# Logits from the unnormed residual, four largest marked by matching, and the first expert's rows gathered in float32

## The chip, the cores and the metric

The kernel runs on one core of one Trainium2 chip. The metric is the device time of one execution in microseconds. The engines are PE (TensorE, matmuls; PEld is its weight load), DVE (VectorE), ACT (ScalarE), POOL (GpSimd) and SP (SyncE, which here issues the large loads). Line numbers L… are those of the kernel before unless "of after" is said.

## What is computed

One block with 256 tokens of width 1024, all in float32: embedding layer norm, a mixer of three branches (sparse attention, S5 scan, attention to a memory) whose gated sum goes through w_o, a DeepNorm residual with layer norm, a mixture of 32 experts of which each token takes four, and a second residual with layer norm. The part that the change touches, in the reference, shortened:

```python
h = _layer_norm(DEEPNORM_ALPHA * h + mix, ln1_g[l], ln1_b[l])
...
logits = xt @ w_router + b_router
top_val, top_idx = lax.top_k(logits, TOP_K)
gate = jax.nn.softmax(top_val, axis=-1)
...
g, lin = jnp.split(xb @ w_gate_up[e] + b_gate_up[e], 2, axis=-1)
act = min(g, 7) * sigmoid(1.702 * min(g, 7)) * (clip(lin, -7, 7) + 1)
y = act @ w_down[e] + b_down[e]          # weighted by gate, summed per token
...
h = _layer_norm(DEEPNORM_ALPHA * h + ffn, ln2_g[l], ln2_b[l])
```

The expert weights are 32 × (8 + 4) MB: the bulk of all that is read.

## The kernel before

**Tiles.** The 256 tokens are two tiles (t = 0, 1) of 128 rows, one token to a partition; the width of 1024 is 8 k-tiles of 128 columns. `h` [128, 2, 1024] holds the residual stream, and is also the accumulator `acc` of the experts.

**Weights.** They come as chunks of 1 MB, [128, 2048] float32. An expert has 8 chunks of w_gate_up and 4 of w_down, 384 in all. Chunks and large intermediate tiles share slots of 8 KB a partition in four pools (tags u, w, s, z with 13, 3, 4 and 4 slots; `PATTERN` says which tag the next chunk takes, `WHERE` where a large tile goes). All loads are issued on SP's queue in program order (L76), so a load whose slot is still in use stops every load behind it. The intermediates `xT1` (transposed rows for the router), `r` (remainder of the split, below) and `l1s` (gain and bias of the layer norm, spread) lie in slots of tag s, and `hb01` in one of tag z, and so each of them delays the chunk that takes its slot next. Some chunks are loaded ahead of the routing (`load_some`).

**Order.** The code is written engine by engine in program order, and a tile scheduler reorders within what the dependencies allow; `issue_after` holds a group of instructions back until a named one stands.

**Before the experts.** `project` multiplies the merged mixer output with w_o into PSUM banks `pz` (L203 to L205, products of the parts hl, mgTh, mgTl, into which both operands are split). The spreads (L141, L913) put the norm's gain and bias on all partitions as `l1s`. Then, for each tile: the residual is added (L921), statistics are taken (L922 to L925, `inv_sqrt` L108 to L117 is a Newton iteration on DVE), h is normalised in place on DVE (L928), 8 transposes (L224) and a copy give `xT1`, and the router multiplies: 8 float32 matmuls with the router weights as the stationary operand in strips of 32 columns (L935), a copy (L938), one matmul by `stack` that adds the strips (L940), and the bias (the norm's gain and bias are folded into the router weights beforehand).

**Routing.** L946 to L953: the eight largest by max, their positions by max_index, a uint32 to float32 cast (L948), a comparison with `eio` (0 to 31) for the first four, and a sum over the four: `sel`, and `selb` in bf16. A matmul by a triangular matrix `before` (L957), for tile 1 with one by ones (L956) ahead of it, counts the earlier tokens of each expert; `posm` (L959, L960) is a token's slot in its expert, or a large number where it isn't marked. Beside it: softmax of the four (`e`, L964 to L967), put in place by `eq` (`gmat`, L969), and `count`, the number of tokens of each expert (L983, L984).

**The split.** h is split into three bf16 parts that add up to it: hi = bf16(h) and mid = bf16(h − hi) on ACT (L977), with r = h − hi and the last part by subtractions of which the first is on DVE and three on POOL (`SUBS`, "VGGG"). The parts lie in `hb01` (hi and mid), `hb2` and the end of the tile `bias`.

**One expert** (`expert`, 64 slots): one-hot `oh` and `og` from posm (L1020, L1021); 48 bf16 matmuls (8 k-tiles, 3 parts, 2 token tiles) gather its rows transposed into PSUM `xg` (L1028); a multiplication on DVE and an addition on POOL apply the layer norm's gain and bias (`xT`); `pw`, `ohT` and `gs` (L1038 to L1042) serve the way back; bias products with `sel` (L1049, L1089); up (L1049, 8 chunks, into pg and pl), swiglu, transposes, down (L1094, 4 chunks), and the combination into acc (L1109, added on DVE). An expert's gathers stand on PE ahead of the up products of the expert before.

**Callbacks.** Expert 0 calls `residual` once xT is written: h is multiplied by alpha and by l1s's gain, and its bias added (L988 to L993, four pieces each). Expert 1 calls `further_blocks`: from `count` it works out how many further blocks of 64 slots an expert needs (`nblk`, L998 to L1003), which each engine, SP among them, reads into a register (TENSOR_LOAD, L1163) to branch over the extra blocks.

Of the kernel before, what the change touches and what calls it, by code (L numbers as in the profile page):

```python
# [52 lines left out]
SUBS = "VGGG"  # L53
L1B = ["mm", "sc", "mm", "sc"]
# [4 lines left out]
def block_kernel(ctx: ExitStack, tc: tile.TileContext, a: dict, out: bass.AP):  # L59
# [33 lines left out]
    G.iota(slot, pattern=[[0, 2], [1, CAP]], base=0, channel_multiplier=0, allow_small_or_imprecise_dtypes=True)  # L93
    posm = cp.tile([128, NT, NE], F32)
# [6 lines left out]
    late = cp.tile([128, 1], F32)  # L101

# [76 lines left out]
    with ExitStack() as fx:  # L179
# [587 lines left out]
        tt(brt, brt, pb_[:, :NE], OP.add)  # L767

# [90 lines left out]
        eio = fp.tile([128, NE], F32)  # L859
        G.iota(eio, pattern=[[1, NE]], base=0, channel_multiplier=0, allow_small_or_imprecise_dtypes=True)  # L860
# [54 lines left out]
        for t in range(NT):  # L915
            zt = h[:, t, :]
            hs = [(slice(n * 512, (n + 1) * 512), zt[:, n * 512:(n + 1) * 512]) for n in range(2)]

            bs = f2.tile([128, 2, 6], F32, tag="bs", name="bs")
            for n, (sl, zh) in enumerate(hs):  # L920
                V.scalar_tensor_tensor(zh, pz[t][n], 0.5 / ALPHA, zh, op0=OP.mult, op1=OP.add)  # L921
                V.bn_stats(bs[:, n, :], zh)  # L922
            mv = f2.tile([128, 2], F32, tag="mv", name="mv")
            V.bn_aggr(mv, bs.rearrange("p a b -> p (a b)"))
            V.tensor_scalar(mv[:, 1:2], mv[:, 1:2], LN_EPS / ALPHA ** 2, None, op0=OP.add)  # L925
            rs = inv_sqrt(f2, mv[:, 1:2])
            for sl, zh in hs:
                V.tensor_scalar(zh, zh, mv[:, 0:1], rs, op0=OP.subtract, op1=OP.mult)  # L928
            transpose_rows(zt, xT1, t, tag="mm" if t else "tr", eng=V if t else None)


            p = bank("mm" if t else "tr")
            for k in range(KT):
                j = k % 4
                PE.matmul(p[32 * j:32 * j + 32, :128], wr[:, k, :], xT1[:, k, t * 128:(t + 1) * 128],  # L935
                          start=k < 4, stop=k >= 4)
            lt = f2.tile([128, 128], F32, tag="lt", name="lt")
            S.activation(lt, p[:, :128], AF.Copy)  # L938
            p = bank("mm" if t else "tr")
            PE.matmul(p[:, :NE], lt, stack, start=True, stop=True)  # L940
            lgt = f2.tile([128, NE], F32, tag="lgt", name="lgt")
            tt(lgt, p[:, :NE], brt, OP.add)
            v8 = f2.tile([128, 8], F32, tag="v8", name="v8")
            i8 = f2.tile([128, 8], U32, tag="i8", name="i8")
            f8 = f2.tile([128, 8], F32, tag="f8", name="f8")
            V.max(v8, lgt)  # L946
            V.max_index(i8, v8, lgt)
            V.tensor_copy(f8, i8)  # L948
            eq = f2.tile([128, 4, NE], F32, tag="eq", name="eq")
            sel = f2.tile([128, NE], F32, tag="sel", name="sel")  # L950
            tt(eq, eio[:, None, :].to_broadcast([128, 4, NE]), f8[:, 0:4, None].to_broadcast([128, 4, NE]), OP.is_equal)
            V.tensor_reduce(sel, eq.rearrange("p k e -> p e k"), axis=AX.X, op=OP.add)
            V.tensor_copy(selb[:, t, :], sel)  # L953
# [5 lines left out]
            V.scalar_tensor_tensor(posm[:, t, :], sel, -1e6, p[:, :NE], op0=OP.mult, op1=OP.add)  # L959
            V.tensor_scalar(posm[:, t, :], posm[:, t, :], 1e6, None, op0=OP.add)  # L960

            e4 = f2.tile([128, 4], F32, tag="e4", name="e4")
            nm = f2.tile([128, 2], F32, tag="nm", name="nm")
            V.tensor_scalar(nm[:, 0:1], v8[:, 0:1], -1.0, None, op0=OP.mult)  # L964
            S.activation(e4, v8[:, 0:4], AF.Exp, bias=nm[:, 0:1], accum_out=nm[:, 1:2])
            V.reciprocal(nm[:, 1:2], nm[:, 1:2])
            V.tensor_scalar(e4, e4, nm[:, 1:2], None, op0=OP.mult)  # L967
            tt(eq, eq, e4[:, :, None].to_broadcast([128, 4, NE]), OP.mult)
            V.tensor_reduce(gmat[:, t, :], eq.rearrange("p k e -> p e k"), axis=AX.X, op=OP.add)  # L969


        for t in range(NT):
            zt, rt = h[:, t, :], r[:, t, :]
# [36 lines left out]
    def expert(mp, pm, gu, dn, pick_e, pos_e, gate_e, slots, then=None, last=None, after=None):  # L1010
# [22 lines left out]
        if then:  # L1033
            then(xT[:, KT - 1, 0:1])
# [265 lines left out]
```

## Time and profile before

| what | us |
|---|---|
| three runs | 1274.22, 1274.98, 1280.77 |
| median | 1274.98 |
| profiled execution, device time | 1278.62 |
| its span in the trace | 1276.9 |
| PE busy in the span | 1217.3 (95%) |
| DVE, ACT, POOL busy | 582.5, 283.5, 63.3 |

The profiled execution is the one that the rows of the trace tell of; it took 3.64 us longer than the median, and 1.7 us of its device time lie outside the span. Times in rows are microseconds from the span's start. Each timeline row gives start, busy time, engine, line, operation, what is written and read, tile shapes, and in brackets how long the engine had been idle before it and what ended that wait. SPq rows are load issues. Equal rows that lie close together are counted as x2, x4 and so on.

### The profile page before, as it was taken

The page shows a single profiled execution, that of the slowest core. Times are in us where ns is not written, and L with a number is a line of the kernel's source. Part 1 is how long each engine was busy: PE and PEld are TensorE (multiplying, and loading weights), DVE is VectorE, ACT ScalarE, POOL GpSimd, SP SyncE. Part 2 cuts the span into 40 slices and gives each one's busy share as a digit, 9 for nine tenths or more (in the row PEclk, how much of TensorE's full clock was granted, in tenths as well). Part 3 has the DMA queues.
Part 4 walks back from the last instruction along what each step waited for, and adds up shares of the span by engine and source line. Part 5 has one row for each costly group of instructions (what it writes and reads, how often), then busy time and mean ns, then how long its engine had stood idle before and what let it go on. Part 6 is the DMA issues. An engine that isn't in the chain of part 4 may idle for free. (4 is left out here: it accounts for less than half of the span.)

```text
span 1276.9 us, 17711 instructions
## 1 busy us (share of the span) xinstructions
PE 1217.3 (95%) x7277; PEld 616.7 (48%) x7278; DVE 582.5 (46%) x1168; ACT 283.5 (22%) x513; POOL 63.3 (5%) x104
## 2 busy tenths in 40 slices
PE   7999999999799999999999999999999999999995
PEld 6657898789533343444444444433333333333341
DVE  5599986657733343333433333333333333333325
ACT  4346469864201110000101001001100000001011
POOL 1000000000200000000000000000000000000000
PEclk9999989999799999999999999999999999999998
DMA  7335546447789999999999999999999999999993
GB/s 273 109 126 198 180 151 215 165 148 282 296 360 427 427 426 427 426 427 426 426 426 427 426 427 425 427 426 427 428 427 425 427 426 427 426 427 427 426 427 143
DMA packets 65333, 451.95 MB, mean 354 GB/s; under 512 B 8896, under 2 KB 9056, under 8 KB 11360
## 3 DMA queue, kind: packets, MB, share of 16 engines
q1 hardware_dynamic: 64960, 450.26, 85.7%
q8 instruction: 58, 0.95, 0.3%
q10 hardware_dynamic: 288, 0.52, 0.1%
q14 instruction: 27, 0.22, 0.0%
HBM read 449.70 MB, written 1.05 MB: 353 GB/s over the span
## 5 line engine op out<-in xcount | busy, mean ns | idle before, releaser
L1049 PE MATMUL pg<-w,xT 128*64 128x512 f32 x1024 | 294.0, 605 | 8.0 <-DMA w<-in_w_gate_up 8.0
L1049 PE MATMUL pl<-w,xT 128*64 128x512 f32 x1024 | 285.6, 592 | 0.0
L1094 PE MATMUL py<-w,aT 128*64 128x512 f32 x1024 | 240.5, 598 | 15.8 <-DMA w<-in_w_down 15.8
L80 DVE TENSOR_TENSOR h<-h,pc 128x512 f32<-128x512 f32 x128 | 82.2, 683 | 267.4 <-PE pc L1109 267.4
L1049 PEld LDWEIGHTS pl<-w,xT 128*64 128x64 f32 x1024 | 95.4, 137 | 126.7 <-issue 103.4
L1069 ACT ACTIVATE sg<-gc 128x512 f32<-128x512 f32 x32 | 20.2, 630 | 560.6 <-DVE gc L1068 560.6
L1094 PEld LDWEIGHTS py<-w,aT 128*64 128x64 f32 x1024 | 69.6, 136 | 154.0 <-issue 100.3
L1049 PEld LDWEIGHTS pg<-w,xT 128*64 128x64 f32 x1024 | 75.3, 136 | 119.6 <-DMA w<-in_w_gate_up 54.7
L1101 DVE SCALAR_TENSOR_TENSOR ys<-py,gs,ys 128x512 fp32r<-128x512 f32 x64 | 48.0, 751 | 166.0 <-ACT ys L1100 162.6
L1100 ACT ACTIVATE ys<-py,gs 128x512 fp32r<-128x512 f32 x64 | 44.0, 687 | 240.6 <-PE py L1094 240.6
L1109 PE MATMUL pc<-ys,ohT 128*128 128x512 f32 x256 | 77.0, 422 | 0.9 <-DVE h L80 0.8
L1109 PEld LDWEIGHTS pc<-ys,ohT 128*128 128x128 f32 x256 | 42.9, 188 | 57.8 <-issue 50.7
L191 DVE TENSOR_TENSOR hl<-w,hl 128x1024 fp32r<-128x1024 f32 x48 | 58.1, 1219 | 17.7 <-ACT hl L190 17.5
L83 POOL TENSOR_TENSOR xT<-xT,lc 128x512 f32<-128x512 f32 x32 | 41.3, 1291 | 472.3 <-DVE xT L80 472.3
L1028 PEld LDWEIGHTS <-hb 128*128 128x128 bf16 x1280 | 47.3, 98 | 30.2 <-issue 28.3
L205 PE MATMUL mm<-hTh,hl 128*128 128x256 f32 x192 | 56.3, 293 | 0.0
L203 PE MATMUL mm<-hTh,hl 128*128 128x256 f32 x192 | 56.2, 293 | 0.0
L204 PE MATMUL mm<-hTl,hl 128*128 128x256 f32 x192 | 55.7, 290 | 0.0
L1068 DVE TENSOR_SCALAR gc<-pg 128x512 f32<-128x512 f32 x32 | 22.1, 691 | 69.9 <-PE pg L1049 69.9
L190 ACT ACTIVATE hl<-w 128x1024 fp32r<-128x1024 f32 x48 | 49.8, 1053 | 18.1 <-PE mm L205 12.5
L1028 PE MATMUL xg<-oh,hb 128*128 128x64 bf16 x1280 | 52.3, 194 | 1.5 <-DVE oh L1020 0.9
L1041 DVE TENSOR_SCALAR ohT<-pw 128x256 fp32r<-128x256 f32 x32 | 13.6, 424 | 71.0 <-PE pw L1038 71.0
(396 smaller groups left out, 1484.0 us busy)
## 6 DMA issues: line engine op xcount, KB each, us to landing
w<-in_w_gate_up SPq DMA_DIRECT2D x256, 1024.0 KB, 19.6
w<-in_w_down SPq DMA_DIRECT2D x128, 1024.0 KB, 19.6
w<-in_w_g SPq DMA_DIRECT2D x12, 1024.0 KB, 4.9
w<-in_w_s_glu SPq DMA_DIRECT2D x4, 1024.0 KB
w<-in_w_o SPq DMA_DIRECT2D x4, 1024.0 KB, 4.7
w<-in_w_memk SPq DMA_DIRECT2D x2, 1024.0 KB, 10.7
w<-in_w_u SPq DMA_DIRECT2D x2, 1024.0 KB, 8.9
w<-in_w_memv SPq DMA_DIRECT2D x2, 1024.0 KB, 5.1
```

The source lines that it names most:

```text
L80: V.tensor_tensor(o, x, y, op=op)
L190: S.activation(hi, src, AF.Copy)
L191: (eng or V).tensor_tensor(lo, src, hi.bitcast(F32), op=OP.subtract)
L203: PE.matmul(o, lhsT(0), rhs(0), start=start, stop=False)
L204: PE.matmul(o, lhsT(0), rhs(1), start=False, stop=False)
L205: PE.matmul(o, lhsT(1), rhs(0), start=False, stop=stop)
L1028: PE.matmul(xg[:, k, :], hb[t][b][:, k * 128:(k + 1) * 128], oh[:, t, :], start=n == 0, stop=n == 5)
L1049: m = PE.matmul(p_[hf * 64:(hf + 1) * 64, :], lhsT, w[:, o + hf * 512:o + (hf + 1) * 512], start=start, stop=stop)
L1094: end = PE.matmul(py[j * 64:(j + 1) * 64, :], a4[:, k // 4, k % 4 + j, :], dn(k + j, hf), start=k + j == 1, stop=k == 6)
L1100: S.activation(y2[:, 0], py, AF.Copy, scale=gs)
L1101: V.scalar_tensor_tensor(y2[:, 1], py, gs, y2[:, 0].bitcast(F32), op0=OP.mult, op1=OP.subtract)
L1109: PE.matmul(pc, ohT[:, t * 128:(t + 1) * 128], ys[hf][:, i], start=i == 0, stop=i == 1)
```

## The change

**Logits.** The residual add, transposes, copy and router products now go by halves of 512 columns (`half(t, n)`), on the residual that isn't normalised yet, with xT1 as the stationary operand (128 columns) and the router weights moving (32 columns): 8 matmuls of 128x32 a tile into one bank `raw`, no strips and no `stack` product. `route(t)` applies mean and deviation to the logits: (raw − mean · swr) · rs + brt, where swr, made once beforehand, holds the column sums of the router weights on all partitions. h is normalised in place by ACT. Tile 0's halves stand between the projections of tile 1, tile 1's first half between those of its second.

**Marking.** max gives the eight largest; match_replace puts 3e38 where one of the first four stands (the eight slots are filled up with −3e38, which the four columns beyond the 32 logits hold), and a comparison gives `selb` at once. `slot` is 1e6 smaller, so that posm needs no second operation.

**What moved behind.** `gates` (softmax over the marked logits) is issued behind expert 0's one-hots. `residual`, issued behind expert 0's last gather matmul, now also allocates r, hb01 and l1s, makes the three bf16 parts (for experts 1 to 31; ACT copies, all four subtractions on DVE) and the spreads of l1s. `further_blocks` counts the marked tokens itself, behind expert 1's gather.

**Expert 0's rows** are gathered from h in float32: 16 matmuls (8 k-tiles, 2 token tiles) with h as the stationary operand, into xg and one `pc` bank; the gain and bias are applied by DVE (k-tiles 0 to 3) and ACT (4 to 7). The down bias products of every expert stand behind its transposes.

SP's queue around the routing: loads of weight chunks, with the semaphores that each waits for (DMAHW: an older load has landed; PE, DVE, Pool, Activation: that engine's last use of the slot). Before, from the 18th chunk on:

```order
89 L76 DMA w<-in_w_gate_up 128x2048 [waits DMAHW3_49]
90 L76 DMA w<-in_w_down 128x2048 [waits DVE_49,DMAHW4_49,PE_49,Activation_49]
91 L76 DMA w<-in_w_down 128x2048 [waits DMAHW5_49,Pool_49]
92 L1163 TENSOR_LOAD nblk [waits DVE_49]
93 L1163 ISA x2
94 L76 DMA w<-in_w_gate_up 128x2048 [waits DMAHW6_49,PE_49]
95 L76 DMA w<-in_w_gate_up 128x2048 [waits DMAHW7_49,PE_49]
```

Row 90 takes xT1's slot, row 91 that of r, and row 94 that of expert 0's first chunk. After:

```order
90 L74 DMA w<-in_w_gate_up 128x2048 [waits DMAHW5_49,PE_49]
91 L74 DMA w<-in_w_down 128x2048 [waits DMAHW6_49,DVE_49]
92 L74 DMA w<-in_w_gate_up 128x2048 [waits DMAHW7_49,PE_49]
93 L74 DMA w<-in_w_gate_up 128x2048 [waits DMAHW0_49,PE_49]
94 L74 DMA w<-in_w_gate_up 128x2048 [waits DMAHW1_49,PE_49]
95 L74 DMA w<-in_w_gate_up 128x2048 [waits DMAHW2_49,PE_49]
96 L74 DMA w<-in_w_gate_up 128x2048 [waits DMAHW3_49,PE_49]
97 L74 DMA w<-in_w_down 128x2048 [waits DMAHW4_49,DVE_49,Activation_49]
98 L74 DMA w<-in_w_gate_up 128x2048 [waits DMAHW5_49,PE_49]
99 L74 DMA w<-in_w_down 128x2048 [waits DMAHW6_49,PE_49]
100 L74 DMA w<-in_w_gate_up 128x2048 [waits DMAHW7_49,PE_49]
101 L1210 TENSOR_LOAD nblk [waits DVE_49]
```

Row 90, the 20th chunk, takes the slot of expert 0's first chunk; row 91, the 21st, takes r's slot, now behind DVE; row 97 takes l1s's slot. The read of nblk has moved from behind the 20th chunk to behind the 30th.

DVE's list from expert 0's way back on. Before:

```order
499 L1041 TENSOR_SCALAR ohT<-pw 128x256
500 L1042 TENSOR_REDUCE gs<-pw 128x1
501 L1021 TENSOR_SCALAR og<-slot,posm,gmat 128x128 x2
502 L1020 TENSOR_SCALAR oh<-slot,posm 128x64
503 L988 TENSOR_SCALAR late<-xT 128x1
504 L80 TENSOR_TENSOR xT<-xg,lc 128x512
505 L992 SCALAR_TENSOR_TENSOR h<-h,late,l1s 128x512 x4
506 L1020 TENSOR_SCALAR oh<-slot,posm 128x64 x2
507 L993 SCALAR_TENSOR_TENSOR h<-l1s,h 128x512 x4
```

And after (hb_3131 is hb01, hb_77 is hb2, the third part of tile 0; bias holds that of tile 1):

```order
487 L995 TENSOR_SCALAR late<-xT 128x1
488 L1086 TENSOR_SCALAR ohT<-pw 128x256
489 L1087 TENSOR_REDUCE gs<-pw 128x1
490 L1051 TENSOR_SCALAR og<-slot,posm,gmat 128x128 x2
491 L78 TENSOR_TENSOR r<-h,hb_3131 128x1024 x2
492 L1008 SCALAR_TENSOR_TENSOR h<-h,l1s 128x512
493 L78 TENSOR_TENSOR hb_77<-r,hb_3131 128x1024
494 L1008 SCALAR_TENSOR_TENSOR h<-h,l1s 128x512
495 L78 TENSOR_TENSOR bias<-r,hb_3131 128x1024
496 L1008 SCALAR_TENSOR_TENSOR h<-h,l1s 128x512 x2
497 L1009 SCALAR_TENSOR_TENSOR h<-l1s,h 128x512 x4
```

Before, DVE has no part of the split here, and expert 1's xT (row 504) stands in between; after, the four subtractions are interleaved with l1s's products, and expert 1's rows come later.

PE's list of after from the last projection products to the first expert weights:

```order
1177 L208 MATMUL av<-hl,mgTl 128x512
1178 L927 MATMUL mm<-ident,h 128x128 x4
1179 L933 MATMUL sc<-s_w_router,xT_2867 128x32 x8
1180 L927 MATMUL mm<-ident,h 128x128 x4
1181 L933 MATMUL sc<-s_w_router,xT_2867 128x32 x8
...
1187 L957 MATMUL mm<-selb,before 128x32
1188 L1060 MATMUL xg<-oh,h 128x64 x16
1189 L144 MATMUL pc<-gbin_ln_g,ident 128x128 x4
1190 L1083 MATMUL pw<-ident,og 128x128 x2
...
1199 L1094 MATMUL pg<-w,xT 64x512 x2
```

Before, the same stretch held four spreads, two times 8 transposes, two times 8 router matmuls with a stack product, one gather matmul, and the bias products, and then 47 more gather matmuls of expert 0 and all 48 of expert 1 ahead of the first product with expert weights; now expert 1's gathers stand behind expert 0's up products.

The diff, cut to what the text speaks of:

```diff
-SUBS = "VGGG"
-L1B = ["mm", "sc", "mm", "sc"]
...
+    V.tensor_scalar(slot, slot, -1e6, None, op0=OP.add)
...
+        wrs = fp.tile([128, NE], F32)
+        V.tensor_reduce(wrs, wr.rearrange("p k e -> p e k"), axis=AX.X, op=OP.add)
...
+        PE.matmul(pb_[:, :NE], onesf, wrs, start=True, stop=True)
+        swr = fp.tile([128, NE], F32)
+        S.activation(swr, pb_[:, :NE], AF.Copy)
...
-        for n in range(2):
-            for k in range(2, KT):
-                project(1, n, k)
-        l1s = big("l1s", [128, 4, 512], **at("l1s"))
-        for i in range(4):
-            S.activation(l1s[:, i], spread(gb1, i, bank(L1B[i], BANKS[L1B[i]])), AF.Copy)
...
+        def half(t, n):
+            zh = h[:, t, n * 512:(n + 1) * 512]
+            V.scalar_tensor_tensor(zh, pz[t][n], 0.5 / ALPHA, zh, op0=OP.mult, op1=OP.add)
+            p = bank("mm" if t else "tr")
+            for k in range(4):
+                PE.transpose(p[:, k * 128:(k + 1) * 128], zh[:, k * 128:(k + 1) * 128], ident)
+            S.activation(xT1[:, 4 * n:4 * n + 4, t * 128:(t + 1) * 128], p.rearrange("p (k c) -> p k c", k=4), AF.Copy)
+            V.bn_stats(stats[t][:, n, :], zh)
...
+            for k in range(4 * n, 4 * n + 4):
+                PE.matmul(raw[t][:, :NE], xT1[:, k, t * 128:(t + 1) * 128], wr[:, k, :], start=k == 0, stop=k == KT - 1)
...
+            V.scalar_tensor_tensor(lgt, swr, nmr[:, 0:1], raw[t][:, :NE], op0=OP.mult, op1=OP.add)
+            V.scalar_tensor_tensor(lgt, lgt, rs, brt, op0=OP.mult, op1=OP.add)
...
+                S.activation(zh, zh, AF.Identity, scale=rs, bias=nmr[:, 1:2])
+            V.max(top[t][:, 0:8], lgt)
...
+            V.match_replace(mark, top[t].rearrange("p (a b) -> p a b", b=4)[:, 0:3:2, :], lg[t], 3e38)
+            V.tensor_scalar(selb[:, t, :], mark[:, :NE], 3e38, None, op0=OP.is_equal)
...
+        for k in range(2, KT):
+            project(1, 0, k)
+        for n in range(2):
+            half(0, n)
+        route(0)
+        for k in range(2, 5):
+            project(1, 1, k)
+        half(1, 0)
+        for k in range(5, KT):
+            project(1, 1, k)
+        half(1, 1)
+        route(1)
...
     def residual(x):
-        V.tensor_scalar(late, x, ALPHA, ALPHA, op0=OP.min, op1=OP.max)
+        r = big("r", [128, NT, D], **at("r"))
+        hb01 = big("hb01", [128, 2, NT, D], BF, tag="z", bufs=NZ)
...
+        V.tensor_scalar(late, x, 1.0, 1.0, op0=OP.min, op1=OP.max)
         for t in range(NT):
             zt, rt = h[:, t, :], r[:, t, :]
...
+            S.activation(hb[t][0], zt, AF.Copy, scale=late)
+            tt(rt, zt, hb[t][0], OP.subtract)
+            S.activation(hb[t][1], rt, AF.Copy)
+            tt(hb[t][2], rt, hb[t][1], OP.subtract)
+        l1s = big("l1s", [128, 4, 512], **at("l1s"))
+        for i in range(4):
+            S.activation(l1s[:, i], spread(gb1, i, pm.tile([128, 512], F32, tag="pc", name="pc", bufs=2)), AF.Copy)
...
+        if first:
+            xg1 = pm.tile([128, 512], F32, tag="pc", name="xg", bufs=2)[:, :256].rearrange("p (k c) -> p k c", k=4)
+            for k in range(KT):
+                o = xg[:, k, :] if k < 4 else xg1[:, k - 4, :]
                 for t in range(NT):
-                    PE.matmul(xg[:, k, :], hb[t][b][:, k * 128:(k + 1) * 128], oh[:, t, :], start=n == 0, stop=n == 5)
+                    after = PE.matmul(o, h[:, t, k * 128:(k + 1) * 128], oh[:, t, :], start=t == 0, stop=t == 1)
...
         if then:
-            then(xT[:, KT - 1, 0:1])
+            with tc.issue_after(after.ins):
+                then(xT[:, KT - 1, 0:1])
```

More of the change, by code (lines that the diff above doesn't have):

```diff
@@ L101, in block_kernel @@
     late = cp.tile([128, 1], F32)
+    one = cp.tile([128, 1], F32)
+    G.memset(one, 1.0)
+    lg = [cp.tile([128, NE + 4], F32, name=f"lg{t}") for t in range(NT)]
+    top = [cp.tile([128, 12], F32, name=f"top{t}") for t in range(NT)]
     def inv_sqrt(st, v, n=1):
@@ L929, in block_kernel @@
[L929 to L953, printed above, removed]
+            lgt = lg[t][:, :NE]
+            V.scalar_tensor_tensor(lgt, swr, nmr[:, 0:1], raw[t][:, :NE], op0=OP.mult, op1=OP.add)
+            V.scalar_tensor_tensor(lgt, lgt, rs, brt, op0=OP.mult, op1=OP.add)
@@ L966, in block_kernel @@
-            V.reciprocal(nm[:, 1:2], nm[:, 1:2])
-            V.tensor_scalar(e4, e4, nm[:, 1:2], None, op0=OP.mult)
-            tt(eq, eq, e4[:, :, None].to_broadcast([128, 4, NE]), OP.mult)
-            V.tensor_reduce(gmat[:, t, :], eq.rearrange("p k e -> p e k"), axis=AX.X, op=OP.add)
+            V.scalar_tensor_tensor(posm[:, t, :], selb[:, t, :], -1e6, p[:, :NE], op0=OP.mult, op1=OP.add)
+        for k in range(2, KT):
+            project(1, 0, k)
+        for n in range(2):
+            half(0, n)
@@ new lines, in block_kernel, with gates @@
+        route(0)
[6 more added lines that the diff above has]
+        route(1)
+    hb = []
+    def gates(mp):
+        w = mp.tile([128, 512], F32, tag="lin", name="ex", bufs=1).rearrange("p (i e) -> p i e", e=NE)
+        for t in range(NT):
+            ex, sel, nm = (w[:, 3 * t + i, :] for i in range(3))
+            V.tensor_scalar(nm[:, 0:1], top[t][:, 0:1], -1.0, None, op0=OP.mult)
+            S.activation(ex, lg[t][:, :NE], AF.Exp, bias=nm[:, 0:1])
+            V.tensor_scalar(sel, posm[:, t, :], 0.0, None, op0=OP.is_lt)
+            tt(ex, ex, sel, OP.mult)
+            V.tensor_reduce(nm[:, 1:2], ex, axis=AX.X, op=OP.add)
+            V.reciprocal(nm[:, 1:2], nm[:, 1:2])
+            V.tensor_scalar(gmat[:, t, :], ex, nm[:, 1:2], None, op0=OP.mult)
@@ L981, in block_kernel @@
-        p = bank("tr")
-        for t in range(NT):
-            PE.matmul(p[0:1, :NE], onesb[:, 0:1], selb[:, t, :], start=t == 0, stop=t == 1)
-        V.tensor_copy(count, p[0:1, :NE])
-    def residual(x):
-        V.tensor_scalar(late, x, ALPHA, ALPHA, op0=OP.min, op1=OP.max)
+            S.activation(hb[t][0], zt, AF.Copy, scale=late)
[3 more added lines that the diff above has]
+        l1s = big("l1s", [128, 4, 512], **at("l1s"))
@@ L995, in further_blocks @@
     def further_blocks(x):
+        p = pm.tile([128, 512], F32, tag="pc", name="pc", bufs=2)
+        w = mp.tile([128, 512], F32, tag="lin", name="pick", bufs=1).rearrange("p (i e) -> p i e", e=NE)
+        for t in range(NT):
+            sel = w[:, t, :]
+            V.tensor_scalar(sel, posm[:, t, :], 0.0, None, op0=OP.is_lt)
+            PE.matmul(p[0:1, :NE], one, sel, start=t == 0, stop=t == 1)
+        V.tensor_copy(count, p[0:1, :NE])
         for b in range(3):
@@ L1087, in down @@
             pys = [pm.tile([128, 512], F32, tag=f"py{i}", name="py", bufs=1) for i in range(2)]
-            for hf, py in enumerate(pys):
-                PE.matmul(py[0:64, :], sel, bias[:, 2 * DFF + hf * 512:2 * DFF + (hf + 1) * 512],
-                          start=True, stop=False)
+            with tc.issue_after(ats[1].ins):
+                for hf, py in enumerate(pys):
+                    PE.matmul(py[0:64, :], sel, bias[:, 2 * DFF + hf * 512:2 * DFF + (hf + 1) * 512],
+                              start=True, stop=False)
             for k in range(0, KT, 2):
```

85 lines of the change are left out of this document (46 added, 39 removed).

## The prediction

> **What bounds the kernel now.** First view: stretches of the whole span (columns: length, then busy time and count of PE, PE's weight loads, DVE, ACT and POOL, granted clock, DMA share, GB/s), then the stream cut in two.
>
> ```profile
> 0.00:340.00 340.00, 326.67 (x1993) 255.07 (x1994) 252.66 (x563) 196.09 (x377) 12.44 (x39) 0.97 0.54 195
> 340.00:356.00 16.00, 10.86 (x129) 6.24 (x131) 13.01 (x46) 1.24 (x4) 5.56 (x7) 0.73 0.44 149
> 356.00:1256.00 900.00, 873.63 (x5136) 353.33 (x5134) 303.03 (x529) 84.82 (x131) 45.34 (x58) 1.00 1.01 425
> 1256.00:1277.00 21.00, 6.13 (x26) 2.08 (x22) 13.79 (x33) 1.37 (x2) 0.00 (x0) 0.75 0.14 55
> 356.00:806.00 450.00, 448.12 (x2758) 190.31 (x2755) 158.36 (x283) 42.72 (x66) 24.69 (x32) 1.00 1.01 426
> 806.00:1256.00 450.00, 425.51 (x2380) 163.02 (x2381) 144.66 (x247) 42.10 (x66) 20.65 (x26) 1.00 1.00 424
> ```
>
> From 356 to 1256 the DMA share is 1.01: the 16 DMA engines never rest. PE has no slack in the first half (448.12 of 450) but 24.5 us in the second, so it catches up with the weights there and then waits for them; the groups of instructions say so too:
>
> ```profile
> L1049 PE MATMUL pg<-w,xT 128*64 128x512 f32 x1024 | 294.0, 605 | 8.0 <-DMA w<-in_w_gate_up 8.0
> L1094 PE MATMUL py<-w,aT 128*64 128x512 f32 x1024 | 240.5, 598 | 15.8 <-DMA w<-in_w_down 15.8
> ```
>
> So the end is set by the weight stream: 384 chunks of 1.0486 MB, at 425 GB/s 2.47 us each. What the change can move is **the moment at which that stream becomes continuous**, less what lies before it. The third view, the 4 us windows around the routing, shows the stream's last hole, and SP's queue (issue start, duration) with its waits shows who makes it.
>
> ```profile
> 329.00:333.00 4.00, 3.93 (x40) 2.82 (x38) 3.71 (x14) 3.50 (x8) 0.00 (x0) 0.81 1.00 412
> 333.00:337.00 4.00, 3.12 (x26) 2.19 (x18) 2.62 (x9) 2.20 (x7) 3.26 (x2) 0.50 1.01 428
> 341.00:345.00 4.00, 0.30 (x2) 0.08 (x1) 3.94 (x15) 0.39 (x2) 2.11 (x1) 0.50 0.80 274
> 345.00:349.00 4.00, 3.67 (x42) 2.27 (x43) 2.08 (x14) 0.00 (x0) 0.92 (x4) 0.56 0.57 236
> 349.00:353.00 4.00, 3.36 (x74) 2.43 (x72) 3.42 (x10) 0.00 (x0) 1.34 (x2) 1.00 0.02 4
> 353.00:357.00 4.00, 4.00 (x20) 1.29 (x18) 4.00 (x8) 0.00 (x0) 1.18 (x1) 1.00 0.49 170
> ```
>
> ```profile
> 343.14 0.33 SPq L76 DMA_DIRECT2D w<-in_w_down  x1
> 353.80 3.76 SPq L76 DMA_DIRECT2D w<-in_w_gate_up  x3
> ```
>
> ```profile
> SPq L76 <- PE pl L1049: 13.2, 7, 5.7
> ```
>
> The 20th chunk is issued at 343.14; the 21st, first of expert 1, needs a slot of expert 0's first chunk and stands until PE has multiplied with it, 353.80. From about 347.3 to 355.05 (the window 353 to 357 has share 0.49, so 1.95 us of transfer before 357) nothing moves. 364 chunks follow without a gap. A microsecond taken off 353.80 is a microsecond off the end, and one put on it is one lost.
>
> Why is PE's release so late? These rows of the timeline are the chain.
>
> ```profile
> 326.80 0.39 PE L205 MATMUL av<-hl,mgTl 128*128 128x512 f32 x1
> 327.57 0.68 DVE L921 SCALAR_TENSOR_TENSOR h<-av,h 128x512 f32<-128x512 f32 x1
> 330.66 1.27 PE L224 MATMUL tr<-ident,h 128*128 128x128 f32 x8
> 331.98 0.16 DVE L117 SCALAR_TENSOR_TENSOR nr_y<-nr_w,nr_y 128x1 f32<-128x1 f32 x1
> 334.27 1.95 PE L224 MATMUL mm<-ident,h 128*128 128x128 f32 x8
> 340.54 0.19 DVE L80 TENSOR_TENSOR lgt<-mm,s_b_router 128x32 f32<-128x32 f32 x1 [0.32 <-PE mm L956]
> 341.29 1.84 DVE L948 CAST f<-i 128x8 f32<-128x8 uint32 x1
> 343.91 0.17 DVE L953 CAST selb<-sel 128x32 bf16<-128x32 f32 x1
> 345.33 0.21 PE L1028 MATMUL xg<-oh,hb 128*128 128x64 bf16 x1 [0.90 <-DVE oh L1020]
> 346.32 1.06 PE L1089 MATMUL py<-bias,sel 128*64 128x512 bf16 x2
> 349.38 0.30 PE L1038 MATMUL pw<-ident,og 128*128 128x128 f32 x1
> 351.82 1.08 PE L1049 MATMUL pg<-w,xT 128*64 128x512 f32 x4
> ```
>
> The projection is done at 327.2, tile 1's logits come at 340.5, the first gather at 345.3, the first product with expert weights at 351.8, and the release of their first chunk 2.0 us later.
>
> **The change part by part.**
>
> *Front, 0 to 327.* The edits there are wrs and swr (one reduction, one matmul, one ACT copy, far from the end of the gate work) against two removed constants; PE is busy 326.67 of 340 and its list is only reshuffled. I take 0. The scheduler may still move it; ±3 us, about 1% of the stretch, is the bound I keep.
>
> *Projection to tile 1's logits.* PE now does tile 0's 8 transposes (1.27 us) before the projection's last products, and no longer needs the four spreads before it. Projection end 327.2 + 1.3 = 328.5, of which I let half a transpose pass, 0.6, fall into PE's waits: 327.9 (327.2 to 328.5). Then the second half's residual add 0.68, 328.6; from there the deviation needs what it needed before (add over at 328.25, last Newton step over at 332.14: 3.9 us), so 332.5. Beside it PE's 4 transposes (0.16 to 0.24 each), an ACT copy, and 16 router passes with 128-column weights: by the row 177.78 below 0.14 each, 2.3 us, ready about 332.4 as well. Two small DVE operations: logits at **333.4** (332.7 to 334.0) in place of 340.7. Normalise, second transpose pass, stack matmul are gone.
>
> *Logits to first gather.* max, match_replace and a compare (0.2 us each; match_replace isn't in this trace, the two operations of max_index, 0.09 and 0.18, are nearest; 0.1 to 0.8) take the place of index, cast, compare and sum. The uint32 cast alone took 1.84 us beside a POOL subtraction. From selb to the gather the old rows give 345.33 − 343.91 = 1.4. Sum with gaps 2.6 us: first gather at **336.0**, 9.3 earlier. The softmax, the count and og lie beside the gather.
>
> *The gather in float32.* 16 matmuls, each two passes on the chip (the 8 router matmuls of before ran as x16), with 128-column float32 weights: 32 passes. Three rows bound a pass.
>
> ```profile
> 175.85 1.99 PE L631 MATMUL tr<-cv,wide 16*128 16x64 f32 x16
> 177.78 3.15 PE L644 MATMUL sc<-ckT,qq 64*128 64x15 f32 x22
> 349.03 0.31 PE L1028 MATMUL xg<-oh,hb 128*128 128x64 bf16 x5
> ```
>
> At full clock 0.124 (x32: 4.0 us), at 0.14 4.6 us, and at the 0.244 that the eight half-clock transposes of 334.27 show, 7.8 us. A bf16 pass of before took 0.06 at most. The clock in the windows is 0.50 from 333 to 345, when PE has little large work. I take 0.16, between the second row and the cold one: 5.0 us, gather over at **341.0** (339.7 to 343.8). The Trainium skill (TensorE: Matmul & The Clock Gate, Weight-path perf modes) speaks against this edit: the fast weight load, about twice as quick, is for types other than float32. The trace agrees: 0.06 for a bf16 pass with its load against 0.12 and more. By its figure for a plain load, columns over 1.2 in ns, a pass would be estimated at 107 ns, and the gather at 3.4 us.
>
> xT's affine, now on DVE and ACT, takes about 0.5 (341.5). PE meanwhile does l1s's first spread (8 passes at 0.124) and pw (2 × 0.30), 1.6: 342.6. Four bias products at 0.53 each, half of one hidden, end at 344.3: PE starts on expert weights 7.5 earlier than before and would release the first chunk at 346.3.
>
> *Who issues the 21st chunk.* This step decides. In SP's list of before (shown with the change) row 91 is the 20th chunk, behind POOL's last read of r, and row 94 the 21st, behind PE. In the list of after the 20th chunk, row 90, waits for PE (346.3), and the 21st stands in row 91 behind r's last read, which has moved from before the gather into `residual` behind it, and from POOL to DVE; everything later on SP's queue stands with it. In DVE's list of after that read is row 495, behind ohT, gs, og, two subtractions for r, the one into hb and two of l1s's products (488 to 494). Durations are in these rows of before:
>
> ```profile
> 330.15 1.22 DVE L80 TENSOR_TENSOR r<-h,hb 128x1024 f32<-128x1024 f32 x1
> 350.35 0.42 DVE L1041 TENSOR_SCALAR ohT<-pw 128x256 fp32r<-128x256 f32 x1
> 350.69 0.41 DVE L1042 TENSOR_REDUCE gs<-pw 128x1 f32<-128x256 f32 x1
> 351.02 0.72 DVE L1021 TENSOR_SCALAR og<-slot,posm,gmat 128x128 f32<-128x128 f32 x2
> 352.53 3.52 DVE L992 SCALAR_TENSOR_TENSOR h<-h,late,l1s 128x512 f32<-128x512 f32 x4
> ```
>
> ```profile
> L190 ACT ACTIVATE hl<-w 128x1024 fp32r<-128x1024 f32 x48 | 49.8, 1053 | 18.1 <-PE mm L205 12.5 <-DMA w<-in_w_g 5.5 <-DMA w<-in_w_o 0.2
> ```
>
> pw is done at 342.6. Then ohT, gs, og: 344.2. Two subtractions for r (ACT makes the two bf16 halves at 1.05 each from 341.6 to 343.7): 346.6. h·l1s at 3.52/4, the next subtraction, h·l1s, the last subtraction: 0.88 + 1.22 + 0.88 + 1.22 = 4.2, 350.8, less some 0.4 by which neighbours overlap on DVE in the rows above: **r free at 350.4**. Bounds: logits and gather at their low ends and h·l1s behind the subtractions, 350.4 − 0.7 − 1.0 − 1.6 = 347.1; gather at half clock and ACT in the chain once more, 354.3. The 20th chunk's load (346.3 + 1.25 + 2.47 = 350.0) is hidden in front of it, so 20 chunks have moved in either kernel when the stream becomes continuous, and the rest is a shift: 350.4 − 353.80 = −3.4 us (−6.7 to +0.5).
>
> *Later.* The count waits in row 101, nine chunks on, when expert 1's positions have long been there; l1s is made in pieces between expert 0's matmuls, which PE's 7.5 us lead covers; if that is gone, PE still has the 24.5 us of the second half. Nothing else is on the stream's path.
>
> **The sum.** The profiled run took 1278.62 (span 1276.9), −3.4 gives 1275.2. That run lies 3.64 above the median of 1274.98 (1274.22 to 1280.77), so on the median's scale **1271.6**. A measurement here tells 0.5%, 6.4 us, from no change; the forecast itself, 0.27%, is within it.
>
> **The rivals.**
> - *r comes free earlier (0.25).* The logits come at 332.7, the 32 passes run at the warm 0.124, and r is free at 347.1 to 348. For it: the clock falls within the window 329 to 333 (0.81, so at about 331.5), some 4.5 us after the last large product at 327, and the new gather starts 9 us earlier. Stream −6.5: 1268.5; with 3 us off the front as well, 1265.5.
> - *Cold gather (0.15).* At 0.244 a pass r is free at 353.2: −0.6, 1274.4. For it: in the new kernel, too, PE has only transposes and thin products between 328 and the gather. The Trainium skill's clock gate (TensorE: Matmul & The Clock Gate, Part 1) would have PE at half rate after an idle window of about 3.4 us; the fall 4.5 us after the last large product agrees with it roughly.
> - *The load queue stands behind `residual` for longer than it stood for PE (0.10, the other side).* Place: SP's row 91, with all later loads behind it. If ACT's four copies and DVE's four subtractions alternate in place of overlapping, each waiting for the other, 4 × 1.05 comes into the chain: 354.6. It decides from r free later than 353.80, a us per us. Alone it gives +0.8, 1275.8; on a cold gather 357.4, +3.6, 1278.6. Against it: two of the copies lie beside ohT, gs and og, and the third beside h·l1s.
> - *PE, not the stream, sets the end.* Then the 7.5 us of earlier start would show whole, 1267.5. The waits of 15.8 and 8.0 us for weights speak against it; its chance, under 0.02, is in the first rival's.
>
> **How the numbers follow.** Forecast (r free 349 to 352.5) 0.50, early 0.25, cold 0.15, late 0.10. The range goes from 1265.0, the early case with the front's gain, to 1278.6, the late one on a cold gather; outside lie the forecast's and the cold case's tails with a front of ±3 and the spread between runs, under 2 in 10. Faster by over 0.5% means below 1268.6: two thirds of the early case, 0.17, and a seventh of the forecast, with a front gain of 2 to 3 us, 0.07: 0.24. Slower means above 1281.4: half of the late case with a front loss of 3, 0.06. Same 0.70.
>
> **What would show it.** In the changed profile: logits of tile 1 near 333.4, first gather near 336, 32 passes of 0.12 to 0.24; SP's 21st issue released by DVE's subtraction into bias near 350, not by PE; the DMA share at 1.00 from about 351.7; the end shifted by as much. It is wrong if the stream becomes continuous with PE's release (then r was early), if SP's wait there names nblk or l1s, or if the stretch before 327 has moved by more than 3 us.

## The result and the profile after

The changed kernel takes 1292.3 us (median of 1290.27 to 1295.78, 4 runs) against 1274.6 for the kernel before (1273.07 to 1280.77): a ratio of 1.0133, 95% interval 1.0093 to 1.0172. It was forecast at 1271.6, between 1265.0 and 1278.6. It is 17 us slower, outside the range and on the other side.

First the stretches of the whole span of the changed kernel, in the columns of the prediction.

```profile
326.00:340.00 14.00, 11.91 (x80) 11.42 (x78) 9.44 (x54) 5.62 (x10) 0.63 (x3) 0.76 0.96 378
340.00:356.00 16.00, 16.00 (x69) 8.30 (x70) 9.75 (x15) 7.27 (x11) 0.00 (x0) 0.78 0.56 218
356.00:806.00 450.00, 446.71 (x2796) 192.52 (x2794) 159.58 (x291) 42.58 (x65) 25.91 (x34) 1.00 1.01 419
806.00:1256.00 450.00, 421.50 (x2344) 157.88 (x2340) 141.01 (x241) 40.92 (x64) 20.69 (x26) 1.00 1.01 419
1256.00:1291.00 35.00, 17.55 (x72) 6.32 (x70) 17.86 (x39) 3.33 (x5) 0.00 (x0) 0.83 0.35 140
```

The last two columns of the third and fourth rows hold the result. The DMA engines are as busy as before (share 1.01), but in the same 450 us they move 419 GB/s in place of 426. 364 chunks are 381.7 MB: 896 us at 426, 911 at 419. **15 of the 17 us are a slower stream**, not a later one. PE shows a part of it: its waits for weights have grown by 5.3 us, from 8.0 and 15.8 us to 11.4 and 17.7 in the groups of instructions.

```profile
L1094 PE MATMUL pg<-w,xT 128*64 128x512 f32 x1024 | 292.8, 608 | 13.0 <-DMA w<-in_w_gate_up 11.4
L1141 PE MATMUL py<-w,aT 128*64 128x512 f32 x1024 | 241.7, 599 | 18.5 <-DMA w<-in_w_down 17.7
```

The start of the stream, on which the prediction spent nearly all of its working, came out much as forecast. SP's issues and its waits around expert 0, and the chain in the timeline:

```profile
347.86 0.33 SPq L74 DMA_DIRECT2D w<-in_w_gate_up  x1
351.14 0.33 SPq L74 DMA_DIRECT2D w<-in_w_down  x1
```

```profile
SPq L74 <- PE pl L1094: 15.3, 1, 15.3
SPq L74 <- DVE bias L78: 2.9, 1, 2.9
```

```profile
327.31 0.39 PE L208 MATMUL av<-hl,mgTl 128*128 128x512 f32 x1
332.40 0.25 DVE L944 SCALAR_TENSOR_TENSOR lg<-lg,nr_y,s_b_router 128x32 f32<-128x32 f32 x1
334.39 7.06 PE L1060 MATMUL xg<-oh,h 128*128 128x64 f32 x32 [0.76 <-DVE oh L1046]
344.86 1.92 PE L1094 MATMUL pg<-w,xT 128*64 128x512 f32 x4
349.90 1.22 DVE L78 TENSOR_TENSOR bias<-r,hb 128x1024 bf16<-128x1024 f32 x1
```

The 21st chunk is issued at 351.14, released by DVE's subtraction into bias (`DVE bias L78`), as the prediction had it (350.4). Logits and gather come earlier than forecast, and the gather itself takes 7.06 us, 0.22 a pass: the rival's price (0.244), not the forecast's (0.16). The granted clock (1.00 is full speed) in the windows agrees, 0.50 to 0.54 from 333 to 345:

```profile
333.00:337.00 4.00, 2.79 (x14) 2.64 (x13) 3.38 (x24) 0.99 (x3) 0.63 (x3) 0.54 1.02 428
341.00:345.00 4.00, 4.00 (x19) 2.88 (x20) 1.05 (x4) 3.29 (x6) 0.00 (x0) 0.50 0.37 152
345.00:349.00 4.00, 4.00 (x16) 1.10 (x12) 4.00 (x6) 2.79 (x4) 0.00 (x0) 0.75 0.08 10
349.00:353.00 4.00, 4.00 (x22) 2.31 (x22) 3.41 (x5) 0.87 (x2) 0.00 (x0) 1.00 0.77 281
```

So two questions are open: why the stream is slower, and what a start that came 2.7 us earlier (351.14 against 353.80) is worth.

### The profile page after: what moved, and what is told of

It is laid out like the page before. It is cut to its first block, busy times and chain, and to the rows that moved or that the text cites. A ratio compares the mean times of both kernels' runs of the same rounds, so it can differ in the third digit from the quotient of the medians.

```text
span 1290.7 us, 17685 instructions
## 1 busy us (share of the span) xinstructions
PE 1225.6 (95%) x7261; PEld 623.2 (48%) x7262; DVE 579.6 (45%) x1170; ACT 285.6 (22%) x514; POOL 55.7 (4%) x104
## 5 line engine op out<-in xcount | busy, mean ns | idle before, releaser
L1094 PE MATMUL pg<-w,xT 128*64 128x512 f32 x1024 | 292.8, 608 | 13.0 <-DMA w<-in_w_gate_up 11.4
L1141 PE MATMUL py<-w,aT 128*64 128x512 f32 x1024 | 241.7, 599 | 18.5 <-DMA w<-in_w_down 17.7
L78 DVE TENSOR_TENSOR h<-h,pc 128x512 f32<-128x512 f32 x128 | 82.2, 684 | 294.9 <-PE pc L1156 294.9
L1071 PE MATMUL xg<-oh,hb 128*128 128x64 bf16 x1240 | 49.7, 193 | 0.0
L1071 PE MATMUL xg<-oh,bias 128*128 128x64 bf16 x248 | 44.2, 193 | 0.0
## 6 DMA issues: line engine op xcount, KB each, us to landing
w<-in_w_memk SPq DMA_DIRECT2D x2, 1024.0 KB, 10.2
```

The source lines that it names most:

```text
L78: V.tensor_tensor(o, x, y, op=op)
L1071: PE.matmul(xg[:, k, :], hb[t][b][:, k * 128:(k + 1) * 128], oh[:, t, :], start=n == 0, stop=n == 5)
L1094: m = PE.matmul(p_[hf * 64:(hf + 1) * 64, :], lhsT, w[:, o + hf * 512:o + (hf + 1) * 512], start=start, stop=stop)
L1141: end = PE.matmul(py[j * 64:(j + 1) * 64, :], a4[:, k // 4, k % 4 + j, :], dn(k + j, hf), start=k + j == 1, stop=k == 6)
```

## The experiments

**Theory A: where the slots start.** The diff adds the constants `one`, `lg0`, `lg1`, `top0` and `top1` to the pool that lies ahead of the slots: 32 + 2 × 160 + 2 × 64 = 480 bytes a partition, as the allocator rounds them to 32. The lowest slot of 8 KB starts at 6656 before (13 × 512) and at 7136 after, 480 past a multiple of 512, and so do all the others. No list of instructions shows this. **Theory B, the rival:** the new order of the work disturbs the stream. The kernels e1 to e4 and f4 tell the two apart; each has the instructions of its parent, as many of each kind on every engine. In the traces of e1 and e2 at most 16 records of an engine stand some places away from where the parent has them.

e1, the changed kernel with 32 bytes more:

```diff
     late = cp.tile([128, 1], F32)
+    pad = cp.tile([128, 8], F32)
```

> The changed kernel with an unused constant of 32 bytes a partition ahead of the slots, so that every slot starts at a multiple of 512 bytes again (before: 6656, changed: 7136 = 13*512+480 for the lowest); the instructions are the same in the same order on every engine. Theory A (where the slots start sets the rate of the weight stream): 425 to 427 GB/s in the stream in place of 419, so about 16 us less, 1271 to 1276 us, and the 3 us earlier restart of the stream shows against the kernel before. Theory B (the changed order of work disturbs the stream: gathers of each expert at other places, down bias products behind the transposes): still 419 GB/s and 1290 to 1294 us.

Measured: 1275.21 us, ratio to the kernel before 1.0004 (0.9991 to 1.0016). All 17 us are gone with the padding, the 2 that the 364 chunks don't explain too, and PE's waits for weights are back at 8.4 and 12.8 us. Its stream:

```profile
356.00:806.00 450.00, 448.59 (x2815) 196.10 (x2815) 160.92 (x293) 44.47 (x68) 25.88 (x34) 1.00 1.01 426
```

e2, the kernel before with 32 bytes fewer ahead of the slots:

```diff
     slots = ctx.enter_context(tc.tile_pool(name="slots", bufs=1))
+    cp2 = ctx.enter_context(tc.tile_pool(name="cp2", bufs=1))
...
-    late = cp.tile([128, 1], F32)
+    late = cp2.tile([128, 1], F32)
```

> The kernel before with the constant late (32 bytes a partition) allocated behind the slots in place of ahead of them: every slot starts 480 bytes past a multiple of 512, as in the changed kernel; instructions and their order are those of before. Theory A: 419 GB/s and 364 chunks at 2.50 in place of 2.46 us, 1288 to 1292 us. Theory B: 427 GB/s, 1273 to 1277 us.

Measured: 1289.98 us, ratio 1.0113 (1.0098 to 1.0128):

```profile
356.00:806.00 450.00, 444.70 (x2734) 185.03 (x2728) 155.55 (x275) 41.91 (x64) 24.70 (x32) 1.00 1.01 419
```

The stream's rate follows the start of the slots and not the order of the work: padding takes the whole loss away from the changed kernel, and moving one constant of 4 bytes gives it to the kernel before. Theory B falls.

e3 (before with `pad` of 32 bytes), e4 (before with `posm` behind the slots) and f4 (before with `count` behind them) ask which boundary it is. Each was measured in one execution.

> The kernel before with 32 unused bytes ahead of the slots: they start 32 past a multiple of 512. Theory A has two forms. A1: any start that is no multiple of 64, 128, 256 or 512 costs the same (one more piece for each 8 KB row), 419 GB/s, 1288 to 1292 us. A2: the price is the bytes between the start and the 256-byte boundary below it (7 x 32 for the changed kernel, 32 here): a seventh of it, about 426 GB/s, 1276 to 1278 us. Theory B: 427 GB/s, as before.

Measured: 1292.71 us.

```profile
356.00:806.00 450.00, 446.18 (x2735) 187.33 (x2732) 158.01 (x280) 41.91 (x64) 24.70 (x32) 1.00 1.01 419
```

> The kernel before with the constant posm (256 bytes a partition) allocated behind the slots: they start 256 past a multiple of 512. If the boundary that matters is 256 bytes or less: 427 GB/s and 1273 to 1277 us. If it is 512: slower, 419 GB/s or in between, above 1280 us. Theory B: as before.

Measured: 1275.26 us.

```profile
356.00:806.00 450.00, 448.12 (x2754) 190.86 (x2752) 156.89 (x277) 43.85 (x67) 24.68 (x32) 1.00 1.01 426
```

> The kernel before with the constant count (128 bytes a partition) allocated behind the slots: they start 384 past a multiple of 512, so 128 past one of 256 and at a multiple of 128. If a multiple of 128 or 64 is enough: 426 GB/s, 1273 to 1278 us. If it takes a multiple of 256: 419 GB/s, 1288 to 1292 us.

Measured: 1287.81 us.

```profile
356.00:806.00 450.00, 446.09 (x2734) 187.12 (x2730) 155.46 (x275) 41.92 (x64) 24.73 (x32) 1.00 1.01 421
```

A start at a multiple of 256 is enough, one at a multiple of 128 isn't, and 32 past costs as much as 480 past: form A1, with e3 0.7 us above its range. f4, 384 past, moves 421 GB/s and lies 0.2 us below that range. The Trainium skill (DMA: Bandwidth & Descriptors, How a descriptor splits into AXI transactions) has the boundary: a descriptor moves in transactions of 256 bytes, and where it doesn't start at a multiple of 256 the first transaction starts at the boundary below, so that the bytes ahead of the start are fetched and unused. It tells this of what a transaction reads; what moved here is the place written. The runs agree on the 256. They don't agree with its price in beats of 32 bytes: estimated by it, a row of 8192 bytes as one descriptor would take 257 beats in place of 256 at 32 past, and 263 at 480 past, while both measured 419 against 426. One transaction more in 32, estimated by the same split, would be 3.1%; measured are 1.7%. Why a start off the boundary costs this much stays open.

**What the aligned change is worth.** With the slots at 512 again the kernel is level with the one before, where −3.4 was forecast. In e1's profile, the last projection product, and the issues of the 20th chunk (released by PE) and the 21st:

```profile
325.60 0.39 PE L209 MATMUL av<-hl,mgTl 128*128 128x512 f32 x1
```

```profile
346.11 0.33 SPq L74 DMA_DIRECT2D w<-in_w_gate_up  x1
349.44 0.33 SPq L74 DMA_DIRECT2D w<-in_w_down  x1
```

From the last projection product to the 21st issue that is 23.8 us. e4 is the kernel before at another address, with the same rate:

```profile
323.32 0.39 PE L206 MATMUL av<-hl,mgTl 128*128 128x512 f32 x1
```

```profile
350.39 0.33 SPq L77 DMA_DIRECT2D w<-in_w_gate_up  x1
```

There it is 27.1 us. So the step between the two moments is worth −3.2 us, but the products end 2.3 us later in e1, and −1.0 us is left at the restart. The kernels that follow are on the wait for r and on the gather's price; all of them have aligned slots.

f1 takes the split out of `residual` and issues it behind the one-hots, so that r is free during the gather:

```diff
             with tc.issue_after(end.ins):
                 gates(mp)
+                split_h()
```

> The aligned changed kernel (e1) with the split of h into bf16 parts taken out of residual and issued behind the one-hots instead, so that ACT and DVE make r and its parts while PE gathers; nothing else changes, and the load of the chunk that takes r's slot now stands ahead of the first one that waits for PE. Theory A (with aligned slots the stream starts with r's last read, 351.1 in the changed kernel, and every microsecond of that is one at the end): r is free by about 342, the load queue's last wait before the stream is PE's release of expert 0's first chunk near 346 to 348, the stream is continuous 2.5 to 3.5 us earlier than in e1: 1272 to 1273 us, ratio to the kernel before about 0.998. Rival (something later than r sets the end, PE or the tail): as e1, 1275 us.

Measured: 1278.51 us, ratio 1.0022 (1.0008 to 1.0035): slower than the kernel before, so both expectations miss. Against e1's 1.0004 (0.9991 to 1.0016) it is higher, though the intervals overlap. The queue's list and its waits say why:

```profile
330.45 12.58 SPq L74 DMA_DIRECT2D w<-in_w_down  x3
354.98 8.43 SPq L74 DMA_DIRECT2D w<-in_w_gate_up  x5
```

```profile
SPq L74 <- PE pl L1097: 11.9, 1, 11.9
SPq L74 <- DVE ex L987: 8.2, 1, 8.2
```

```profile
341.47 1.21 DVE L78 TENSOR_TENSOR bias<-r,hb 128x1024 bf16<-128x1024 f32 x1
350.89 1.07 PE L1097 MATMUL pl<-w,xT 128*64 128x512 f32 x2
354.35 0.59 PE L1097 MATMUL pl<-w,xT 128*64 128x512 f32 x1
```

r is free at 342.7, against 349.4 in e1, and its chunk is loaded; the wait of 8.2 us is that chunk's, put down to an operation of DVE that ended beside r's last read. But the next chunk waits for PE's release of expert 0's first chunk, and that has moved from 346.11 (e1) to 354.98. Of this 3.3 us lie ahead of the change (the last projection product starts at 328.92, in e1 at 325.60); from that product on it is 26.1 us in place of 20.5. The scheduler, with other work ready earlier, put six of expert 1's gathers ahead of the first chunk's products and pw and sixteen spread passes between them, and PE ran at the half clock until about 350.2 (in e1 until 345.2). The wait for r was taken away, and a longer one for PE took its place.

f2 leaves the order of e1 and puts eight products that nobody reads on PE where it waits during the routing (5 ahead of tile 1's counting products and 3 between them):

```diff
         half(1, 1)
+        pw_ = bank("tr")
+        for i in range(5):
+            PE.matmul(pw_, onesb, bias[:, 0:512], start=True, stop=True)
         route(1)
+        pw_ = bank("tr")
+        for i in range(3):
+            PE.matmul(pw_, onesb, bias[:, 0:512], start=True, stop=True)
```

> The aligned changed kernel (e1) with eight unused bf16 products of 128x512 on PE (5 and 3) between the router's last product and the last counting product, where PE waits; their results are read by nobody. Theory A (the gather's 7.06 us, 0.22 a pass, is the half clock, and r's chain hangs on it): a higher granted clock in 333 to 341, the gather at 4 to 5 us, r free 2 to 3 us earlier, less 0.5 for products that come in the way: 1273 us. Rival (a float32 pass costs 0.22 here whatever the clock, or the clock doesn't rise for so few products): gather again 7 us, 1275 to 1276 us.

Measured: 1271.93 us, ratio 0.9974 (0.9960 to 0.9987), the first that beats the kernel before. Its gather, and PE's first release (the first issue of the row):

```profile
332.37 3.76 PE L1067 MATMUL xg<-oh,h 128*128 128x64 f32 x32 [0.78 <-DVE oh L1053]
340.19 5.83 SPq L74 DMA_DIRECT2D w<-in_w_gate_up  x3
```

```profile
333.00:337.00 4.00, 4.00 (x37) 3.93 (x35) 2.56 (x15) 0.93 (x4) 0.00 (x0) 1.00 1.02 430
```

At a clock of 1.00 the same 32 passes take 3.76 us, 0.12 each, in place of 7.06. PE's release comes 15.2 us behind the last projection product, in e1 20.5. The profiled execution took 1268.44 us and is one of five with a mean clock of 0.990 to 0.992 (1268.38 to 1270.78 us); the other six have 0.987 to 0.989 and 1271.93 to 1274.43 us, and whether the clock held through the gather in them isn't known. f3 is both edits.

> Both edits, f1's early split and f2's eight products. Expert 1's gathers now stand ahead of expert 0's first product with weights. Theory A: the gather is over 2 to 3 us earlier, PE's first release at 343 to 346, the stream continuous 4 to 6 us earlier than in e1: 1270 to 1272 us. Rival: as f1 if the clock doesn't rise, 1272 to 1273.

Measured: 1273.76 us, ratio 0.9983 (0.9971 to 0.9995): a little above the range, and above f2. In its profile the first issue that waits for PE's release comes at 345.85, in f2 at 340.19:

```profile
345.85 12.24 SPq L74 DMA_DIRECT2D w<-in_w_gate_up  x6
```

Of these 5.7 us 4.3 lie ahead of both edits, since the last projection product starts at 329.31 (f2: 325.03); from there on it is 16.5 us against 15.2. The clock isn't the same either: in f3 it fell at about 333.6, just ahead of the eight products, which ran at the half clock, and it was back at 1.00 when the gather started at 338.30, which again took 3.76 us:

```profile
333.00:337.00 4.00, 4.00 (x19) 2.25 (x19) 1.97 (x13) 2.57 (x3) 0.00 (x0) 0.58 1.02 430
```

f2 had moved r's chunk two places back in SP's queue as well. Three kernels are to part the two: g1 with four products (lists and queue as in e1), g2 with eight narrow ones (as in e1), g3 with five (queue as in f2).

> The aligned changed kernel (e1) with four unused bf16 products of 128x512 on PE behind tile 0's counting product, where PE waits; apart from these every engine's list is that of e1, the load queue's too (in f2 eight products had also moved r's chunk two places back in it). Theory A (the granted clock of PE during the gather is what costs): if four suffice to keep the clock up, the gather takes 3.8 us as in f2, the spread and pw 1 us less, r is free 3 to 4 us earlier, 1271 to 1273 us; if they don't, the gather stays at 7 us and the time at 1275. Rival (f2's gain is that of the place of r's chunk in the queue): 1275 us even with a gather of 3.8 us.

Measured: 1275.05 us, ratio 0.9994 (0.9980 to 1.0009), gather at half clock:

```profile
332.84 7.06 PE L1064 MATMUL xg<-oh,h 128*128 128x64 f32 x32 [0.77 <-DVE oh L1050]
```

> As f2, but the eight unused products have 8 columns in place of 512 (0.02 to 0.06 us each); the other engines' lists and the load queue are those of e1. Theory A (it is the work of the products that holds the clock): the gather at half clock, 7 us, 1275 us, as e1. Rival (any product on PE in the wait does it): gather 3.8 us, 1271 to 1273.

Measured: 1277.89 us, ratio 1.0006 (0.9991 to 1.0021), gather at half clock too:

```profile
335.14 7.06 PE L1067 MATMUL xg<-oh,h 128*128 128x64 f32 x32 [0.77 <-DVE oh L1053]
```

Eight products of 8 columns didn't hold the clock in this profile, so the work counts and not the number alone. No execution of g1 or g2 has a mean clock above 0.987.

> As f2, with five unused products of 128x512 in place of eight; the lists of the other engines and the load queue are those of f2, in which the chunk that takes r's slot stands two places further back than in e1. If five leave the clock at half (four did), the run tells what the queue's order is worth alone: theory A (the clock is the larger part of f2's gain): gather 7 us, PE's first release at 346 as in e1 and the next chunks behind it, 1273 to 1275 us. Rival (the order is the larger part): 1271 to 1272.5 us with a gather of 7 us. If five keep the clock up, the gather is at 3.8 us and the time as f2's, 1271 to 1272.

Measured: 1273.90 us, ratio 0.9983 (0.9963 to 1.0004), and neither case of the expectation alone. The 12 executions fall into two groups:

| mean granted clock | executions, us |
|---|---|
| 0.989 to 0.992 | 1266.50, 1268.01, 1268.93, 1269.03, 1269.77 |
| 0.982 to 0.987 | 1273.00, 1274.80, 1274.83, 1275.01, 1278.97, 1279.20, 1279.92 |

The profiled one, of the first group (1266.50), has the gather at 3.76 us:

```profile
330.38 3.76 PE L1064 MATMUL xg<-oh,h 128*128 128x64 f32 x32 [0.76 <-DVE oh L1050]
```

Same instructions, same queue: with five products the clock holds in some executions. The median of the others, 1275.0, is e1's time, although the queue is f2's, which suggests that the order of the queue is worth little while the clock is lost. It isn't shown. That the gather ran at half clock in the second group is inferred from their mean clock; none of them was profiled, and the mean also counts a stretch of half clock near 180 us that differs between executions (3.4 us in this profile, 13.6 in f1's). No run has the full clock with e1's queue, so what the order adds there wasn't measured.

h1 puts seven products ahead of tile 1's counting products and four behind them.

> The aligned changed kernel with eleven unused products of 128x512, seven ahead of the counting product of tile 1 and four behind it, in PE's two waits; all other lists are those of f2 and g3. Theory A (whether the clock holds through the gather decides, and with five products it held in some executions only, at a mean granted clock of 0.989 to 0.992 and 1266.5 to 1269.8 us against 0.982 to 0.987 and 1273 to 1279.9): with more work in the waits it holds in nearly all: mean clock 0.989 or more, 1268 to 1271 us, ratio to the kernel before 0.994 to 0.997. Rival (the spread of g3 and f2 comes from elsewhere, start-up for one): the same spread as g3, median 1272 to 1274.

Measured: 1272.93 us, ratio 0.9974 (0.9962 to 0.9985): the ratio is f2's, just above the one forecast, and the median above its range too. One execution of 1532.51 us at a mean clock of 0.748 is left out of the ratio. Of the other eleven, six have the mean clock of 0.989 or more that was forecast for nearly all. The median lies in the rival's range, though the spread, 1270.30 to 1275.53, is narrower than g3's. The profile shows the clock lost in the middle of the gather, at about 334.2 (0.65 in this window):

```profile
331.48 4.65 PE L1069 MATMUL xg<-oh,h 128*128 128x64 f32 x32 [0.55 <-DVE oh L1055]
```

```profile
333.00:337.00 4.00, 4.00 (x25) 3.88 (x24) 1.75 (x8) 0.83 (x3) 0.00 (x0) 0.65 1.00 422
337.00:341.00 4.00, 4.00 (x16) 1.90 (x16) 1.18 (x5) 3.12 (x5) 0.00 (x0) 0.50 0.48 199
```

In this execution eleven products didn't carry the clock through the gather, where in f2's profile eight did, so their number alone doesn't decide it. And the gather, on which PE is busy without a pause, doesn't itself keep the clock up. The best of the kernels run is f2 (with h1 level by ratio): the aligned change with PE kept at work, 0.26% below the kernel before.

## Why the prediction was wrong, point by point

- **The step that failed is the price behind "364 chunks follow without a gap", the 2.47 us a chunk.** There is no gap (the DMA share is 1.01), but each chunk costs more. The prediction took the rate of the stream from the kernel before and let only its start move ("the rest is a shift"). The rate fell from 426 to 419 GB/s, 2.50 us a chunk, which is 15 us of the 17. The part "Front" named wrs, swr and two removed constants and passed over the five new ones: 480 bytes of them moved every slot off its boundary. e1 and e2 show it from both sides. No rival had it.
- **"Projection to tile 1's logits"** was right in kind: the logits come at 332.65, at the lower bound given (332.7) in place of 333.4, and the products ended where forecast (327.7 and 327.9).
- **"Logits to first gather"**: 1.74 us in place of 2.6. max to selb took 0.7 us for the step that had cost 3.3 before.
- **"The gather in float32"** was mis-sized: 7.06 us in place of 5.0. The cold rival's condition came true, and its row (0.244 a pass) was the near one: PE had only transposes and thin products from 327.5 on. 0.16 was chosen between rows of two clocks. The row behind 0.14 (177.78) itself ran at the half clock (0.50 from 180 to 184 in that profile), with 15 moving columns in place of 64, so it was no price for a warm pass; the 32 router passes of the changed kernel, at 1.00, took 0.12 each. f2 and g3 show the gather at full clock, 3.76 us.
- **"Who issues the 21st chunk"** held: r's last read by DVE released it, at 351.14 against 350.4. That it is so near is in part luck. The gather began 1.6 early and was 2.1 long, the spread and pw behind it were 1.0 long at the half clock, and h·l1s was shorter than forecast (0.69 in place of 0.88 each).
- **"−3.4 us"** for the restart: from the last projection product it is −3.2 (27.1 to 23.8, in e4 and e1). But the end of that projection moved by more than the 0.7 us allowed for. In e1 it lies 2.3 us behind e4's, of which one transpose pass is 1.03. The moment isn't fixed without the change either: in the kernel before and its four copies at other addresses (e2, e3, e4, f4) the last product starts at 326.80, 323.05, 326.33, 323.32 and 323.42, and the restart follows 27.0 to 27.4 us later each time. The profiled execution of before was one of the late ones, which made the change look better by up to 3 us in a comparison of profiles. So what the aligned change is worth, a ratio of 1.0004 (0.9991 to 1.0016), is consistent with −3.2 in that step and a loss of a like size ahead of it, but how much of the loss belongs to the change stays open.
- **"Front"**, put at 0 with ±3 us, may well not be 0. On a stretch between 176 and 196 us, with PE busy throughout, the clock is at 0.50 for 3.4 us in g3, 10.2 in e1 and 13.6 in f1, and their last projection products start at 323.30, 325.60 and 328.92. From 180 to 240 the granted clock is 0.89 to 0.97 in the nine profiles of the changed kernel and its variants, and 0.96 to 0.99 in the five of the kernel before and its copies. Why it is lower there, and what it costs, wasn't tested.
- **"The load queue stands behind `residual`"** got the place right and was not what decided: r came free ahead of the 353.80 that the rival needed. f1 shows that with r out of the way PE's release is next, and not for free.

## What to carry to other kernels

When a change adds or drops even a small constant, ask what lies behind it in memory: print the start of the large transfer targets before and after, and keep them at a multiple of 256 bytes, since here 32 bytes decided 1.1 to 1.3% of the time of a kernel that is bound by its loads. A forecast that shifts a saturated stream must also say why its rate stays. And where small float32 products stand in a critical chain after PE's heavy work has ended, price them at the half clock unless a row at that place shows otherwise.

## What the runs showed of the hardware

- The rate of a stream of 1 MB loads (128 rows of 8 KB) into the core's memory by the start of the rows: 426 GB/s at a multiple of 512 and at 256 past one, 421 at 384 past, 419 at 32 and at 480 past. The share of time in which the DMA engines are busy is 1.01 in all, so the share alone doesn't show the loss; the GB/s column does.
- A float32 pass of the gather, with 128-column weights and 64 moving columns, takes 0.12 us at clock 1.00 and 0.22 at 0.50. In e1, g1, g2 and the changed kernel 32 of them in a row, with PE busy throughout, run 7 us without the clock rising, and in h1 it falls while they run. Products of 128x512 in bf16 in the wait ahead of them: four didn't hold the clock in the execution profiled, five and eight did (g3, f2), and with eleven (h1) it fell in the gather.
